# Layer 1 of a two-layer decoder trunk: output projection by token group with Strassen operands made beside it, and the layer-0 handover's operand made in two parts

## The chip, the cores and the metric

The kernel is one program on one core of a Trainium2 chip. The metric is the device time of one execution in microseconds, given as the median of several runs. The engines are TensorE (PE; its weight loads are PEld), VectorE (DVE), ScalarE (ACT), GpSimd (POOL) and SyncE (SP), which issues the DMA transfers.

## The reference

One inference step of a two-layer decoder over 1024 prompt tokens and 64 sample tokens, 1088 in all, width 1024, in float32. What matters here:

```
# layer 0: mixer (causal convolution, stick-breaking attention), FFN
# layer 1: mixer (short gated convolution, causal pooling), FFN
hn  = rms_norm(h, norm_mix_g[1])
mix = concat([c, d]) @ w_out_odd                  # 1024 x 1024, the output projection
h   = h + mix
g, u = split(rms_norm(h, norm_ffn_g[l]) @ w_ffn_in[l])   # 1024 x 2*2816
h   = h + (silu(g) * u) @ w_ffn_out[l]            # 2816 x 1024
y   = rms_norm(h, norm_final_g)
```

## The kernel before

The residual `hb` lies in SBUF as 8 blocks of 128 channels by 1088 tokens. Tokens form group A (`GA`, 0 to 511, one column block of 512), group B (`GB`, 512 to 1087, two of 288) and, in layer 1's mixer, both together (`GT`, blocks of 364, 364 and 360). A float32 product is three matmuls (`mm3`): weight and operand are each a rounded high part and a low part, and the fourth product is dropped. The parts of a weight tile are made as it comes (`w_split`): ACT copies the high part (L177), POOL subtracts for the low part in two halves (L179). Of an operand, ACT makes the high part and DVE the low part (`split`, `prep`, `mix_operand`).

The order on every engine is the program's own. Weights come in the order of the list `seq` through four staging buffers and three buffers `hl`; `w_next` prepares two entries ahead. PSUM holds three accumulators for a single group and two for `GT`. In an FFN, 22 channel groups f are made in pairs, and after each pair from the second on comes the output product of the pair before (eight blocks of 6 matmuls in A, 12 in B, added to `hb` by DVE, L286). The call `slot()` between matmuls is where other work is put in the queues.

A channel group is made in one of two forms. Plain: two products over 8 channel blocks, 48 matmuls in A and 96 in B, with the norm's factor `rr` multiplied in on evacuation (L282). Strassen (`strassen`): seven half-size products for gate and up together, 84 matmuls of 256 or 288 columns, on operands already normed and added ("forms" b11, b21, b22, t1 to t4), and on sums of weight tiles, made by DVE (L193 to L195, L207) and split by ACT and POOL (L189, L190). Here the first five channel groups (`PLAIN`) of three FFNs, layer 0's B and layer 1's A and B, are plain, and `make_forms` makes the forms beside them: DVE norms `hb` (L1372) and takes differences (L1385 to L1388), ACT and POOL split those (L1390, L1391), and `switch` splits the rest with DVE.

The joints that the change touches: `to_mixer` (the last output blocks of layer 0 in group B, with the operand `x1t` of layer 1's mixer made beside them, L1350 and L1352); `run_out` for `GT` (output projection of layer 1, eight groups of 72 matmuls, the last two as a pair, while `prep` makes group A's operand); `channel1` for A, whose last output blocks make group B's operand (`last_a1`); and `channel1` for B. Before the output projection `mix_operand` splits the mixer's output and DMAs the residual back into `hb` from `park`.

Of the kernel before, what the change touches and what calls it, by code (L numbers as in the profile page):

```python
# [8 lines left out]
F = mybir.dt.float32  # L9
# [24 lines left out]
class Grp:  # L34


    def __init__(self, c0, c1, w):
        self.c0, self.c1, self.n, self.w = c0, c1, c1 - c0, w
        self.blocks = [(a, min(a + w, c1 - c0)) for a in range(0, c1 - c0, w)]
        self.t0, self.t1 = c0 // 128, -(-c1 // 128)  # L40
        self.cs = slice(c0, c1)
# [3 lines left out]
GA = Grp(0, HALF, 512)  # L45
GB = Grp(HALF, T, 288)
GT = Grp(0, T, 364)
# [3 lines left out]
def parts(g, acc, *flat):  # L51
    k = sum(b - a == g.w for a, b in g.blocks)
    yield (acc[:, 0:k, :g.w],) + tuple(f[:, 0:k * g.w].rearrange("p (b n) -> p b n", b=k) for f in flat)
    if k < len(g.blocks):
        yield (acc[:, k, :g.n - k * g.w],) + tuple(f[:, k * g.w:g.n] for f in flat)
# [3 lines left out]
def trunk_kernel(ctx, tc, x_prompt, x_sample, cache_k, cache_v, state_conformer, state_shortconv, state_pool,  # L59
# [12 lines left out]

    gstack = ExitStack()
# [12 lines left out]
    par = consts.tile([128, 200], F, name="par")  # L86
# [30 lines left out]
    def add_ffn(l, plain=NF):  # L117
# [13 lines left out]
    PLAIN = 5  # L131
# [14 lines left out]
    for n in range(8):  # L146
        add_in(w_out_odd[0], n * 128)
    for _ in range(2):
        add_ffn(1, PLAIN)

# [110 lines left out]
    def norm_a(g, ps, count):  # L261
        norm_cols(ps, count, g.t0, g.t1)
        k = g.t1 - g.t0
        dg = tmp()
# [104 lines left out]
    def mix_operand(g, x, ks):  # L369
        for c in ks:  # L370
            split(x[c][:, :, :g.n], hb[:, c, g.cs])
# [42 lines left out]
    def run_ffn(g, accs, ps, hidp, x, last, sig=False, slot=lambda: None, forms=None):  # L414
# [3 lines left out]
        gate = {}  # L418

        def ev_g(a):  # L420
            t = tmp()
            scaled(g, t[:, :n], a)
# [7 lines left out]

        def ev_u(f, a):
            t = tmp()
# [3 lines left out]
        def gated(f, t, u):  # L436
            if f // 2 not in hid:
                hid[f // 2] = hidp.tile([128, 2, 2, n], FR, name="hid")
            dst = hid[f // 2][:, f % 2]
# [56 lines left out]
        for q in range(G + 1):  # L496
            if q < G:
                for f in (2 * q, 2 * q + 1):
                    if forms and f >= PLAIN:
                        if f == PLAIN:  # L500
                            forms["switch"]()
                        strassen(f)
                        continue
                    if f == 0:
# [4 lines left out]
                    one(f, 1)  # L509
            if q == G:  # L510
# [53 lines left out]
    x1stack = ExitStack()  # L564
    x1p = x1stack.enter_context(tc.tile_pool(name="x1b", bufs=1, side="right"))
    x1 = [x1p.tile([128, 2, GB.n], FR, name=f"x1_{c}") for c in range(KC)]
# [763 lines left out]
    def to_mixer(hh):  # L1330
        nonlocal x1
        assert not sq and not jobs
        behind = []
        fstack.close()
        x1stack.close()
        gstack.close()
        tmpbox[:] = [tstack.enter_context(tc.tile_pool(name="tmps", bufs=3, side="right")), 1152]
        r1p = r1stack.enter_context(tc.tile_pool(name="r1", bufs=1, side="right"))
        x1 = [r1p.tile([128, 2, T], FR, name=f"x1t_{c}") for c in range(KC)]
        for o in range(2):  # L1340
            h = w_next()
            for i in range(4):
# [404 lines left out]
```

## Time and profile before

| what | us |
|---|---|
| median of 3 runs | 2648.62 (2648.56 to 2649.83) |
| profiled execution, its own time | 2657.19 |
| its span, first to last instruction | 2655.4 |
| TensorE busy in it | 2544.4 |
| DVE, POOL, ACT busy | 1622.3, 1553.1, 1085.1 |

The mean granted clock of TensorE in the profiled execution is 0.985 of full speed. Busy time is an average over stages; what a stage waits for is read in that stage. A matmul lasts longer than the distance to the next, since they are pipelined, so distances are what counts.

### The profile page before, as it was taken

What the parts mean: (1) busy time and instruction counts of PE and PEld (TensorE: products, weight loads), DVE (VectorE), ACT (ScalarE), POOL (GpSimd) and SP (SyncE); (2) the same over time, 40 slices, a digit from 0 to 9 for tenths busy, and PEclk for the clock granted to TensorE, in tenths of its full rate; (3) what the DMA queues carried; (4) which work ended last, traced back from release to release, by engine and by line L of the source; (5) the groups of instructions that cost most, each with busy time, mean ns of one, the idle gap of its engine ahead of it and who ended that gap; (6) DMA issues with size and microseconds to landing.
All of it is one profiled execution on the core that took longest, in us unless ns stands there. A gap on an engine that the chain in (4) does not pass through costs nothing. (4 is left out here: it accounts for less than half of the span.)

```text
span 2655.4 us, 40689 instructions
## 1 busy us (share of the span) xinstructions
PE 2544.4 (96%) x15627; PEld 2263.9 (85%) x15627; DVE 1622.3 (61%) x2262; ACT 1085.1 (41%) x1806; POOL 1553.1 (58%) x1199
## 2 busy tenths in 40 slices
PE   8989999999999999999999999999999998999998
PEld 6788877887666657999999999998788887999997
DVE  4684777868756543377656643332676667676665
ACT  5436766744333324334333421222333334343333
POOL 6756244443333338578787732234778886677775
PEclk9999999999999999999999999999999999999999
DMA  7332231234445442422333321131233333233232
GB/s 215 116 102 71 62 110 40 72 100 129 143 126 161 115 119 88 138 73 80 96 89 87 115 59 48 43 108 40 72 96 96 96 96 94 59 114 107 84 93 76
DMA packets 346009, 254.07 MB, mean 96 GB/s; under 512 B 22657, under 2 KB 295169, under 8 KB 345800
## 3 DMA queue, kind: packets, MB, share of 16 engines
q1 hardware_dynamic: 345784, 251.46, 32.4%
q8 instruction: 124, 2.03, 0.3%
q14 instruction: 69, 0.57, 0.1%
q10 hardware_dynamic: 32, 0.01, 0.0%
HBM read 233.21 MB, written 18.69 MB: 95 GB/s over the span
## 5 line engine op out<-in xcount | busy, mean ns | idle before, releaser
L179 POOL TENSOR_TENSOR hl<-stage,hl 128x512 fp32r<-128x512 f32 x484 | 656.3, 1379 | 485.7 <-ACT hl L177 334.3
L226 PE MATMUL acc<-x,hl 128*128 128x288 f32 (+1 forms) x3792 | 709.8, 340 | 11.8 <-DVE hb L286 7.9
L226 PEld LDWEIGHTS acc<-x,hl 128*128 128x128 f32 x3792 | 585.0, 190 | 98.1 <-issue 38.4
L226 PE MATMUL acc<-hid,hl 128*128 128x288 f32 (+1 forms) x3072 | 554.1, 337 | 26.3 <-DVE tmp L282 13.8
L226 PEld LDWEIGHTS acc<-hid,hl 128*128 128x128 f32 x3072 | 470.1, 191 | 94.4 <-DVE hb L286 15.9
L286 DVE TENSOR_TENSOR hb<-acc,hb 128x512 f32<-128x512 f32 (+2 forms) x376 | 266.7, 718 | 245.8 <-PE acc L226 244.5
L177 ACT ACTIVATE hl<-stage 128x1024 fp32r<-128x1024 f32 x242 | 253.5, 1053 | 213.5 <-PE acc L226 136.8
L463 PE MATMUL acc<-tt,hl 128*128 128x288 f32 (+1 forms) x2448 | 331.6, 291 | 0.5 <-ACT hl L189 0.5
L463 PEld LDWEIGHTS acc<-tt,hl 128*128 128x128 f32 x2448 | 321.0, 189 | 1.7 <-ACT hl L189 0.7
L226 PE MATMUL acc<-x1t,hl 128*128 128x364 f32 (+1 forms) x1728 | 294.7, 332 | 5.5 <-DVE hb L286 5.0
L226 PEld LDWEIGHTS acc<-x1t,hl 128*128 128x128 f32 x1728 | 290.2, 191 | 7.1 <-ACT x1t L1350 5.2
L190 POOL TENSOR_TENSOR hl<-sum,hl 128x512 fp32r<-128x512 f32 x153 | 199.1, 1328 | 158.6 <-ACT hl L189 158.6
L467 DVE TENSOR_TENSOR tmp<-acc,tmp 128x288 f32<-128x288 f32 (+1 forms) x357 | 148.4, 442 | 199.3 <-ACT tmp L479 127.4
L463 PE MATMUL acc<-x,hl 128*128 128x288 f32 (+1 forms) x1836 | 257.1, 292 | 8.3 <-DVE tmp L467 6.5
L463 PEld LDWEIGHTS acc<-x,hl 128*128 128x128 f32 x1836 | 243.8, 190 | 11.2 <-ACT hl L177 5.7
L190 POOL TENSOR_TENSOR hl<-stage,hl 128x512 fp32r<-128x512 f32 x153 | 227.5, 1509 | 18.8 <-ACT hl L189 18.8
L282 DVE TENSOR_TENSOR tmp<-acc,rr 128x512 f32<-128x512 f32 (+3 forms) x128 | 89.6, 711 | 183.0 <-PE acc L226 173.5
L189 ACT ACTIVATE hl<-sum 128x512 fp32r<-128x512 f32 x153 | 87.6, 624 | 209.3 <-DVE sum L195 190.6
L243 POOL TENSOR_TENSOR ss<-ss,tmp 128x512 f32<-128x512 f32 (+2 forms) x62 | 105.7, 1704 | 88.3 <-ACT tmp L242 84.9
L442 POOL TENSOR_TENSOR tmp<-tmp 128x512 f32<-128x512 f32 (+1 forms) x88 | 130.6, 1484 | 24.8 <-ACT tmp L428 23.8
L232 DVE TENSOR_TENSOR hid<-tmp,hid 128x512 fp32r<-128x512 f32 (+1 forms) x88 | 95.7, 1087 | 56.4 <-ACT hid L231 56.0
L226 PE MATMUL acc<-x1a,hl 128*128 128x512 f32 x480 | 122.1, 408 | 3.0 <-POOL hl L179 1.3
(254 smaller groups left out, 2986.7 us busy)
## 6 DMA issues: line engine op xcount, KB each, us to landing
stage<-in_w_ffn_in_dram SPq DMA_DIRECT2D x176, 512.0 KB
stage<-in_w_ffn_out_dram SPq DMA_DIRECT2D x88, 512.0 KB
stage<-in_w_in_even_dram SPq DMA_DIRECT2D x40, 512.0 KB
kst<-in_cache_k_dram SPq DMA_DIRECT2D x64, 256.0 KB
vst<-in_cache_v_dram SPq DMA_DIRECT2D x64, 256.0 KB
stage<-in_w_out_even_dram SPq DMA_DIRECT2D x16, 512.0 KB
stage<-in_w_in_odd_dram SPq DMA_DIRECT2D x16, 512.0 KB
park<-hb SPq DMA_DIRECT2D x16, 288.0 KB
```

The source lines that it names most:

```text
L177: act.activation(hl[:, 0], st, AF.Copy)
L179: pool.tensor_tensor(hl[:, 1, c], st[:, c], f32(hl[:, 0, c]), op=OP.subtract)
L189: act.activation(hl[:, 0, c], x, AF.Copy)
L190: pool.tensor_tensor(hl[:, 1, c], x, f32(hl[:, 0, c]), op=OP.subtract)
L226: pe.matmul(acc[:, b, :c1 - c0], w, x[:, xi, c0:c1], start=first and s == 0, stop=last and s == 2)
L232: dve.tensor_tensor(dst[:, 1], src, f32(dst[:, 0]), op=OP.subtract)
L243: pool.tensor_tensor(ss[:, g.cs], ss[:, g.cs], t[:, :g.n], op=OP.add)
L282: dve.tensor_tensor(d, a, r, op=OP.mult)
L286: dve.tensor_tensor(d, a, d, op=OP.add)
L442: pool.tensor_tensor(t[:, :n], t[:, :n], u[:, :n], op=OP.mult)
L463: pe.matmul(acc[:, :w2], h[:, wi, i, k], xk[:, xi], start=k == 0 and s == 0, stop=k == 3 and s == 2)
L467: dve.tensor_tensor(out, acc[:, :w2], x, op=OP.add)
```

## The change

`GT` gets column blocks of 512, 288 and 288, and an operand of it may be a pair of tiles, one of group A and one of group B (`mm3`, `mix_operand`). At the end of layer 0, group A's part of the mixer's operand is made one output earlier, in the slots of the last output but one (`early`), in memory that the Strassen forms leave; `to_mixer` makes group B's part alone. The output projection of layer 1 runs for group A and then for group B, so its 8 weight tiles are loaded twice. Beside group B's half, `forms_a` norms group A and makes all its forms. Group A's FFN has no plain channel groups; in its slots `forms_b` norms group B, and in its last two outputs `free_a` and `go_on` split that. Group B's FFN has two plain channel groups on that normed operand, without the factor on evacuation (`done`), and the differences are made beside them (`job`).

```diff
-GA = Grp(0, HALF, 512)
-GB = Grp(HALF, T, 288)
-GT = Grp(0, T, 364)
+GA = Grp(0, HALF, (0, 1, 512, 0))
+GB = Grp(HALF, T, (0, 2, 288, 0))
+GT = Grp(0, T, (0, 1, 512, 0), (1, 2, 288, 512))
...
-    for n in range(8):
-        add_in(w_out_odd[0], n * 128)
     for _ in range(2):
-        add_ffn(1, PLAIN)
+        for n in range(8):
+            add_in(w_out_odd[0], n * 128)
+    for _ in range(2):
+        add_ffn(1, PLAIN1[_])
...
+    PLAIN, PLAIN1 = 5, (0, 2)
...
-                pe.matmul(acc[:, b, :c1 - c0], w, x[:, xi, c0:c1],
+                xs, o = (x, 0) if not isinstance(x, tuple) else (x[0], 0) if c0 < x[2] else (x[1], x[2])
+                pe.matmul(acc[:, b, :c1 - c0], w, xs[:, xi, c0 - o:c1 - o],
...
+        done = forms and "switch" not in forms
 
         def ev_g(a):
             t = tmp()
+            if done:
+                for p, o in parts(g, a, t):
+                    act.activation(o, p, AF.Silu)
+                gate["t"] = t
+                return
...
         def ev_u(f, a):
+            if done:
+                t, dst = gate.pop("t"), to_hid(f)
+                for p, o in parts(g, a, t):
+                    dve.tensor_tensor(o, p, o, op=OP.mult)
+                late.append(lambda: split(dst, t[:, :n]))
+                return
...
-                    if forms and f >= PLAIN:
-                        if f == PLAIN:
-                            forms["switch"]()
+                    if f >= plain:
+                        if f == plain:
+                            forms.get("switch", forms.get("ready"))()
                         strassen(f)
                         continue
-                    if f == 0:
+                    if f == 0 and not done:
...
+            if q == G - 1:
+                free()
...
+        x1 = [(x1[c], r1p.tile([128, 2, GB.n], FR, name=f"x1t_{c}"), HALF) for c in range(KC)]
...
-                gain = pc(MIXG + 8 + n)
-                act.activation(x1[n][:, 0], hb[:, n], AF.Copy, scale=gain)
-                for gr in (GB, GA):
-                    lowq.append(lambda gr=gr, n=n, gain=gain: dve.scalar_tensor_tensor(
-                        x1[n][:, 1, gr.cs], hb[:, n, gr.cs], gain, f32(x1[n][:, 0, gr.cs]), op0=OP.mult,
-                        op1=OP.subtract))
-                if n > 1:
-                    behind.append(lowq.pop())
+                prep(GB, [x[1] for x in x1], n, pc(MIXG + 8 + n))
                 low(1)
         low()
-        for f in behind:
-            f()
...
+        ahead = []
+
+        def early():
+            fstack.close()
+            for n in range(KC):
+                def f(n=n):
+                    o, i, gain = x1[n][:, :, :HALF], hb[:, n, GA.cs], pc(MIXG + 8 + n)
+                    act.activation(o[:, 0], i, AF.Copy, scale=gain)
+                    dve.scalar_tensor_tensor(o[:, 1], i, gain, f32(o[:, 0]), op0=OP.mult, op1=OP.subtract)
+                ahead.append(f)
+
         def slot_f():
+            if ahead:
+                return ahead.pop(0)()
...
-    run_out(GT, accs, x1, FFNG + 8, KS, then=(GA, x2))
...
+    def out_fin(g, n, a):
+        added(g, hb[:, n, g.cs], a)
+        add_squares(g, hb[:, n, g.cs], n == 0)
+
+    def normed(out, c, cs, view=lambda ap: ap):
+        dve.scalar_tensor_tensor(out, view(hb[:, c, cs]), pc(FFNG + 8 + c), view(rr[:, cs]), op0=OP.mult, op1=OP.mult)
+
+    def lows(o, src):
+        dve.tensor_tensor(o[:, 1], src, f32(o[:, 0]), op=OP.subtract)
+
+    def sums_t(b11, b12, b21, b22, t1, t2, t3, t4):
+        for o, p, q in ((t1, b12, b11), (t3, b22, b12), (t2, b22, t1), (t4, b21, t2)):
+            dve.tensor_tensor(o, p, q, op=OP.subtract)
+
+    def forms_a(ep):
+        for _ in range(5):
+            yield 1
+        dg = norm_a(GA, ms, D, ep.tile([128, 1024], F, name="fa"))
+        for _ in range(4):
+            yield 1
+        norm_b(GA, ms, dg)
+        for _ in range(2):
+            yield 1
+        w = HALF // 2
+        for k in range(4):
+            fa, fb = (ep.tile([128, 1024], F, name=n) for n in ("fa", "fb"))
+            normed(fa[:, :HALF], k, GA.cs)
+            normed(fa[:, HALF:], k + 4, GA.cs)
+            dsts = ((b1[k][:, :, :w], fa[:, :w]), (b2[k][:, :, :HALF], fa[:, HALF:]),
+                    (xa[k][:, :, :HALF], fb[:, :HALF]), (xa[4 + k][:, :, :HALF], fb[:, HALF:]))
+            for o, i in dsts[:2]:
+                act.activation(o[:, 0], i, AF.Copy)
+            yield 1
+            b11, b12, b21, b22, t2, t1, t4, t3 = (t[:, i * w:i * w + w] for t in (fa, fb) for i in range(4))
+            sums_t(b11, b12, b21, b22, t1, t2, t3, t4)
+            for o, i in dsts[2:]:
+                act.activation(o[:, 0], i, AF.Copy)
+            yield 1
+            yield 1
+            for o, i in dsts:
+                lows(o, i)
+            yield 1
+
+    a0, a1 = pair(GA, accs, xa, KS, {})
+    out_fin(GA, 0, a0)
+    out_fin(GA, 1, a1)
+    for n in range(2, KC):
+        h = w_next()
+        a = accs()
+        block(GA, a, h, xa, KS)
+        out_fin(GA, n, a)
+    with tc.tile_pool(name="fab", bufs=1) as ep:
+        gen = forms_a(ep)
+        for n in range(KC):
+            h = w_next()
+            a = accs()
+            block(GB, a, h, xb, KS, slot=lambda: next(gen, 0))
+            out_fin(GB, n, a)
+            next(gen, 0)
+        for _ in gen:
+            pass
...
+    def forms_b():
+        yield 1
+        dg = norm_a(GB, ms, D)
+        yield 1
+        norm_b(GB, ms, dg)
+        yield 1
+        for k in range(4):
+            normed(xs[k][:, 0:GB.n], k + 4, GB.cs)
+            yield 1
+            normed(xs[k][:, GB.n:], k, GB.cs)
+            yield 1
+
+    def parts_b(k):
+        return [xs[k][:, i * W2:i * W2 + W2] for i in range(4)]
+
+
+    def free_a():
+        def piece(o, i):
+            act.activation(o[:, 0], i, AF.Copy)
+            lows(o, i)
+
+        for k in range(4):
+            seam.append(lambda k=k: piece(b2[k], xs[k][:, 0:GB.n]))
+            seam.append(lambda k=k: piece(b1[k], parts_b(k)[2]))
+
+
+        def last_part(k):
+            if k == 0:
+                rest_b["t"] = hidp1.tile([128, 2, 2, GB.n], FR, name="hid").rearrange(
+                    "p a s (b n) -> p (a s) b n", b=2)
+            piece(rest_b["t"][:, k], parts_b(k)[3])
+
+        for k in range(4):
+            seam.append(lambda k=k: last_part(k))
+
+        def job(k):
+            b21, b22, b11, b12 = parts_b(k)
+            sums_t(b11, b12, b21, b22, b11, b22, b12, b21)
+            for o, x in ((xa[k], xs[k][:, W2:3 * W2]), (xa[4 + k][:, :, R], b12), (xa[4 + k][:, :, L], b21)):
+                act.activation(o[:, 0], x, AF.Copy)
+                pool.tensor_tensor(o[:, 1], x, f32(o[:, 0]), op=OP.subtract)
+
+        jobs.extend(lambda k=k: job(k) for k in range(4))
+
+    def go_on():
+        if seam:
+            seam.pop(0)()
+
+    def ready():
+        while jobs:
+            jobs.pop(0)()
+
+    def channel1(g, last, side, free, plain, x):
+        side = side()
+        turn[0] = 0
+        j0 = wj[0]
...
             turn[0] += 1
-            if turn[0] % 3 == 0:
-                if jobs:
+            if seam:
+                return go_on()
+            if turn[0] % 3 == 0 or turn[0] < 4 and g is GA:
+                if jobs and g is GB:
                     jobs.pop(0)()
-                elif wj[0] > jstart + 2 * PLAIN:
+                elif g is GA or wj[0] > j0 + 2 * plain + 2:
                     next(side, 0)
...
-                prep(GB, x1, n, pc(FFNG + 8 + n))
-                behind.append(lowq.pop())
-                if n < 2:
-                    behind.pop()()
-        for f in behind:
-            f()
-
-
-    def rows_a(fp):
+                go_on()
+        assert not seam
...
+    channel1(GA, last_a1, forms_b, free_a, PLAIN1[0], None)
```

## Rows read from the trace of the kernel before

**Rows 1.** Stretches (us): length, busy of PE, PEld, DVE, ACT, POOL; clock; DMA.

```profile
1508.00:1536.00 28.00, 21.03 (x125) 20.10 (x124) 21.87 (x25) 16.60 (x20) 17.25 (x12) 0.88 0.49 155
1836.00:1856.00 20.00, 16.24 (x67) 12.61 (x66) 7.43 (x15) 6.11 (x9) 10.89 (x6) 0.91 0.18 53
1856.00:1888.00 32.00, 32.00 (x143) 26.50 (x142) 26.51 (x32) 14.04 (x20) 26.57 (x19) 1.00 0.28 82
1888.00:1936.00 48.00, 39.64 (x192) 33.13 (x191) 27.93 (x39) 16.59 (x28) 32.66 (x25) 0.89 0.26 76
2200.00:2224.00 24.00, 18.57 (x67) 13.95 (x67) 15.31 (x16) 7.99 (x12) 10.04 (x9) 0.86 0.29 84
2236.00:2324.00 88.00, 80.35 (x585) 79.20 (x584) 61.35 (x73) 31.18 (x47) 59.40 (x41) 0.98 0.24 69
```

**Rows 2.** VectorE in order of time, layer 0 to 1: start, us, instruction.

```profile
1497.06 0.76 DVE L286 TENSOR_TENSOR hb<-acc,hb 128x576 f32<-128x576 f32 x1 [1.14 <-PE acc L226]
...
1514.59 0.74 DVE L1352 SCALAR_TENSOR_TENSOR x1t<-hb,par,x1t 128x512 fp32r<-128x512 f32 x1
...
1526.66 1.29 DVE L1352 SCALAR_TENSOR_TENSOR x1t<-hb,par,x1t 128x576 fp32r<-128x576 f32 x1
1527.87 0.74 DVE L286 TENSOR_TENSOR hb<-acc,hb 128x576 f32<-128x576 f32 x1
```

**Rows 3.** VectorE's evacuations in layer 1, in order of time.

```profile
1800.65 1.36 DVE L286 TENSOR_TENSOR hb<-acc,hb 128x728 f32<-128x728 f32 x2 [10.64 <-PE acc L226]
...
1920.10 0.69 DVE L282 TENSOR_TENSOR tmp<-acc,rr 128x512 f32<-128x512 f32 x1 [4.75 <-PE acc L226]
...
2312.72 0.76 DVE L282 TENSOR_TENSOR tmp<-acc,rr 128x576 f32<-128x576 f32 x1 [5.64 <-PE acc L226]
```

**Rows 4.** The chain that ended last: start, us, piece.

```profile
2064.16 11.47 PE acc L226 x48
...
2129.81 11.49 PE acc L226 x48
...
2448.30 22.24 PE acc L463 x168
```

**Rows 5.** VectorE in order of time, group A of layer 1.

```profile
1856.12 1.14 DVE L1372 SCALAR_TENSOR_TENSOR xs<-hb,par,rr 128x512 f32<-128x512 f32 x2
...
1882.82 0.42 DVE L1385 TENSOR_TENSOR tmp<-tmp,xs 128x256 f32<-128x256 f32 x1
...
1938.42 0.68 DVE L232 TENSOR_TENSOR hid<-tmp,hid 128x512 fp32r<-128x512 f32 x1
```

**Rows 6.** VectorE by line, 1855 to 1927: busy us, mean ns of one.

```profile
L232 DVE TENSOR_TENSOR x<-xs,x 128x512 fp32r<-128x512 f32 x4 | 4.7, 1232 | 0.0
L1385 DVE TENSOR_TENSOR tmp<-tmp,xs 128x256 f32<-128x256 f32 x4 | 4.6, 1153 | 0.1
...
L1372 DVE SCALAR_TENSOR_TENSOR xs<-hb,par,rr 128x512 f32<-128x512 f32 x4 | 3.4, 848 | 0.0
L1388 DVE TENSOR_TENSOR tmp<-xs,tmp 128x256 f32<-128x256 f32 x4 | 2.7, 671 | 0.1
```

**Rows 7.** GpSimd in order of time, end of group A.

```profile
2193.18 7.55 POOL L179 TENSOR_TENSOR hl<-stage,hl 128x512 fp32r<-128x512 f32 x6
```

**Rows 8.** TensorE in order of time, group A of layer 1.

```profile
1944.76 4.47 PE L463 MATMUL acc<-tt,hl 128*128 128x256 f32 x36
...
1965.12 5.22 PE L226 MATMUL acc<-hid,hl 128*128 128x512 f32 x21
```

**Rows 9.** VectorE in order of time, end of group A.

```profile
2198.31 6.66 DVE L232 TENSOR_TENSOR hid<-tmp,hid 128x512 fp32r<-128x512 f32 x1
```

**Rows 10.** GpSimd by line, 2249 to 2290, start of group B.

```profile
L1391 POOL TENSOR_TENSOR tt<-tmp,tt 128x576 fp32r<-128x576 f32 x8 | 12.3, 1557 | 6.7 <-ACT tt L1390 6.7
```

**Rows 11.** A stretch at the start of the output projection.

```profile
1745.00:1750.00 5.00, 5.00 (x32) 5.00 (x31) 5.00 (x3) 0.00 (x0) 4.41 (x2) 1.00 0.93 326
```

**Rows 12.** VectorE by line, 1935 to 2194, group A's FFN.

```profile
L193 DVE TENSOR_TENSOR sum<-stage 128x512 f32<-128x512 f32 x16 | 32.5, 2031 | 0.0
```

More of the change, by code (lines that the diff above doesn't have):

```diff
@@ L34, with __init__ @@
 class Grp:
-    def __init__(self, c0, c1, w):
-        self.c0, self.c1, self.n, self.w = c0, c1, c1 - c0, w
-        self.blocks = [(a, min(a + w, c1 - c0)) for a in range(0, c1 - c0, w)]
+    def __init__(self, c0, c1, *runs):
+        self.c0, self.c1, self.n, self.runs = c0, c1, c1 - c0, runs
+        self.blocks = [(a + i * w, a + i * w + w) for _, k, w, a in runs for i in range(k)]
         self.t0, self.t1 = c0 // 128, -(-c1 // 128)
@@ L44 @@
 HALF = 512
-GA = Grp(0, HALF, 512)
-GB = Grp(HALF, T, 288)
-GT = Grp(0, T, 364)
+GA = Grp(0, HALF, (0, 1, 512, 0))
+GB = Grp(HALF, T, (0, 2, 288, 0))
+GT = Grp(0, T, (0, 1, 512, 0), (1, 2, 288, 512))
 def parts(g, acc, *flat):
[L52 to L55, printed above, removed]
+    for b, k, w, c in g.runs:
+        yield (acc[:, b:b + k, :w],) + tuple(f[:, c:c + k * w].rearrange("p (b n) -> p b n", b=k) for f in flat)
 @with_exitstack
@@ L70, in trunk_kernel @@
     ctx.enter_context(tc.manual_schedule())
+    x1stack = ExitStack()
+    x1p = x1stack.enter_context(tc.tile_pool(name="x1b", bufs=1, side="right"))
+    x1 = [x1p.tile([128, 2, GB.n], FR, name=f"x1_{c}") for c in range(KC)]
     gstack = ExitStack()
@@ L410, in out_block, with run_ffn @@
             mm3(g, a, h[:, 0, k, i * 128:i * 128 + 128], h[:, 1, k, i * 128:i * 128 + 128], hh[:, k], k == 0, k == 1)
-    def run_ffn(g, accs, ps, hidp, x, last, sig=False, slot=lambda: None, forms=None):
+    def run_ffn(g, accs, ps, hidp, x, last, sig=False, slot=lambda: None, forms=None, plain=NF,
+                free=lambda: None, hw=None):
         G = NF // 2
@@ L436, in gated @@
         def gated(f, t, u):
[L437 to L439 removed]
+            dst = to_hid(f)
             def fin():
@@ L1331, in to_mixer @@
         nonlocal x1
[L1332 to L1335, printed above, removed]
+        assert not sq and not jobs and not ahead
         gstack.close()
+        r1p = r1stack.enter_context(tc.tile_pool(name="r1", bufs=1, side="right"))
+        x1 = [(x1[c], r1p.tile([128, 2, GB.n], FR, name=f"x1t_{c}"), HALF) for c in range(KC)]
         tmpbox[:] = [tstack.enter_context(tc.tile_pool(name="tmps", bufs=3, side="right")), 1152]
-        r1p = r1stack.enter_context(tc.tile_pool(name="r1", bufs=1, side="right"))
-        x1 = [r1p.tile([128, 2, T], FR, name=f"x1t_{c}") for c in range(KC)]
         for o in range(2):
@@ L1424, in trunk_kernel @@
         jstart = wj[0] + 3
-        run_ffn(GB, accs, ms, hidp, x1, to_mixer, slot=slot_f, forms=forms)
+        run_ffn(GB, accs, ms, hidp, x1, to_mixer, slot=slot_f, forms=forms, plain=PLAIN, free=early)
     acc_pool(GT, 2)
@@ L1563, in trunk_kernel @@
+    ystack0 = ExitStack()
+    tstack.close()
     r1stack.close()
[L1564 removed]
+    fp = fstack.enter_context(tc.tile_pool(name="forms1", bufs=1))
     tmpbox[:] = [ystack0.enter_context(tc.tile_pool(name="tmph", bufs=4, side="right")), 640]
[L1566 to L1575 removed]
+    hidp1 = ystack0.enter_context(tc.tile_pool(name="hid1", bufs=2, side="right"))
@@ new lines, in trunk_kernel @@
+    xs = [fp.tile([128, 2 * GB.n], F, name=f"xs{k}") for k in range(4)]
+    L, R = slice(0, W2), slice(W2, GB.n)
+    seam, jobs, rest_b = [], [], {}
+    def forms_b():
[11 more added lines that the diff above has]
+        return [xs[k][:, i * W2:i * W2 + W2] for i in range(4)]
@@ L1589, in end @@
                 pass
-            fstack.close()
+            if g is GB:
+                fstack.close()
             last(hh)
-        run_ffn(g, accs, ms, hidp, x1, end, slot=slot, forms=forms)
-        hstack.close()
+        run_ffn(g, accs, ms, hidp1, x, end, slot=slot, forms=dict(form_views(g.n // 2), ready=ready), plain=plain,
+                free=free, hw=GB.n)
     def last_a1(hh):
-        behind = []
         for o in range(2):
@@ L1706, in to_y @@
         finish(1)
-    channel1(GB, to_y, rows_a)
+    channel1(GB, to_y, rows_a, lambda: None, PLAIN1[1],
+             [(b1[k], rest_b["t"][:, k], W2) for k in range(4)] + b2)
     ystack.close()
```

56 lines of the change are left out of this document (29 added, 27 removed).

## Prediction, made before the changed kernel was run

> **What bounds the kernel now.** I first read busy time and granted clock by stretch. Between the joints TensorE has no idle time: 32.00 of 32.00 us at clock 1.00 in 1856 to 1888 [rows 1]. So the change can win in two ways: fewer or cheaper matmuls, and shorter joints. What a joint loses is its length less busy time times clock: 28 - 21.03 x 0.88 = 9.5 us where layer 0 hands over to layer 1; 20 - 16.24 x 0.91 = 5.2 and 48 - 39.64 x 0.89 = 12.7, together 17.9, where layer 1's FFN starts on group A; 24 - 18.57 x 0.86 = 8.0 at its end; 88 - 80.35 x 0.98 = 9.3 where group B starts [rows 1]. Together 44.7 us. Part of it is clock: at the first joint the idle time is 28 - 21.03 = 7.0, and the other 2.5 us go at the lower of the two levels, 1.2 instead of 2.4 GHz, after the idle time. I then read the engines' instructions in order of time for the price of a column block and for what VectorE (DVE) does at the joints.
>
> **The change part by part**, gains positive.
>
> *A, layer 0 to 1.* Before, ACT makes both groups' operand in the last eight output blocks and DVE its low parts; TensorE's next matmuls need the PSUM tiles that the last add frees. The adds run from 1497.06 to 1527.87 + 0.74 = 1528.6 [rows 2]. After, group A's eight low parts come eight blocks earlier. DVE then has in the first eight blocks 8 adds x 0.68 + 8 low parts x 1.0 (an estimate between 0.74 and 1.29 [rows 2]) + two hidden splits of some 0.75 = 14.9 us, in the last eight, up to the last add, 8 x 0.68 + 6 x 1.1 = 12.0: the last add ends near 1497.1 + 26.9 = 1524.0, 4.6 us earlier, while TensorE's 16 blocks of 12 matmuls need 16 x 6.40/4 = 25.6 [rows 3]. I take 5, with a little of the clock; ends 0 (all low parts at 1.29 push the last add back to 1528) and 9.5 (the whole loss).
>
> *B, column blocks.* 1088 columns become 512 + 288 + 288 for 364 + 364 + 360; the count of matmuls stays. 72 matmuls of the old form took 10.64 + 1.36 = 12.00 us (DVE's idle time until their block ends, and the evacuation, so the time from one to the next), so three take 0.500; 24 of 512 took 4.75 + 0.69 = 5.44, so 0.2267 each; 48 of 288 took 5.64 + 0.76 = 6.40, so 0.1333 each [rows 3]. 0.2267 + 0.2667 = 0.4934, and 576 triples x 0.0066 = 3.8. Ends 0 and, with 22.24/168 = 0.1324 for 288 [rows 4], 4.9.
>
> *C, the start of group A's FFN.* Gone are the pair at the end of the output projection with its operand, the norm that waits for the squares, and the forms made beside five plain channel groups: the 17.9 us. In their place forms_a runs inside group B's half of the projection, 8 x 6.40 = 51.2 us, and the first Strassen product needs all of it. By its yields the first piece stands behind the third add, at 3 x 6.40 + 0.75 = 19.9 us; behind it come 4 x 10 DVE instructions with two SBUF inputs, 3 for the first weight sums, and 5 more adds (3.8): 23.7 us beside the 43. Undisturbed, one k costs 1.14 (two of 512) + 4 x 0.42 + 3 x 0.68 + 0.42 = 5.3 [rows 5]; with POOL 83% busy (26.57 of 32) [rows 1] the same kinds took 2 x 0.848 + 4 x 0.91 (mean of the first and last difference) + 3 x 1.232 + 0.42 = 9.5 [rows 6]. In group B's half POOL has two weight halves and one square, 3 x 1.45 = 4.35 of 6.40 us, 68%, so I interpolate to 8.7 for a k and 1.13 for a weight sum: 34.8 + 3.4 + 23.7 = 61.9, that is 10.7 us after TensorE is done. With 2.5 for the clock, as at the first joint, 17.9 - 13.2 = 4.7 is won. Ends: undisturbed, 21.1 + 2.0 + 23.7 = 46.9 fits and all 17.9 is won; at the full contended price 65.2, 14.0 late, 1.4 won. Queued behind the late forms: on DVE the adds that free PSUM (three buffers, so two blocks or 12.8 us of slack), on ACT the copies that wait for them and behind these the weight copies of two blocks later, on POOL the halves that wait for those.
> Six POOL halves in a row took 7.55 us, 1.26 each [rows 7]. The Trainium skill, SBUF — State Buffer, section "SBUF: two separate sides", says that DVE (with two SBUF inputs) and GpSimd take a shared port pair as an exclusive lock for a whole instruction. By it the times would simply add: 23.1 of DVE + 15 x 1.26 of POOL + 23.7 = 65.7, 14.5 late, and 3.8 less is won than by the rows; the stretch of [rows 6] does not decide it, so it is a rival.
>
> *D, group A's five plain channel groups.* A plain one is 2 x 5.44 = 10.88 [rows 3], two by Strassen in a row took 1965.12 - 1944.76 = 20.36, so 10.18 each [rows 8]: 5 x 0.70 = 3.5. But a round of two Strassen groups and one output takes (2129.81 - 2064.16)/2 = 32.8 [rows 4] against 20.36 + 10.88 = 31.2: 1.6 lost at each output, where weight sums hold DVE. Two outputs more of that kind, less some slack: I take 1; ends -1.3 and 3.5.
>
> *E, the end of group A.* Twelve small copies and subtractions stand in the last two outputs instead of eight wide ones in and behind the last. A two-input split of 0.68 took 6.66 us here [rows 9], against the train of [rows 7], which stays: the same two output and two input weights are prefetched. I leave most of the 8.0 standing and take 2; ends -4 (the twelve at the contended price) and 6.
>
> *F, the start of group B.* Norm and normed operand are already made in group A's time; two plain groups (25.6 us) remain, with four jobs beside them, the last issued some 19 us in. Each has four differences and on POOL three low parts; the 576-wide kind took 1.557 [rows 10], the three about 3.2. With the weights POOL has about 4 x 3.2 + 12 x 1.4 = 29.6 us for 25.6. The forms may be late by 0 to 4; I take 3 of the 9.3 as staying: 6; ends 0 and 9.3.
>
> *G, group B's three plain ones.* 2 x 6.40 = 12.8 against 22.24/2 = 11.12 [rows 3, 4]: 3 x 1.68 = 5.0.
>
> *H, at nothing or nearly.* Eight more weight loads: one ACT copy and two POOL halves (2.5) for 5.44 us of TensorE, covered; without cover 2.5 each. The restored residual is needed sooner: the DMA engines are 93% busy there [rows 11], the first add comes 10.9 us after the first matmul, and three PSUM buffers give 10.9 more; a late one costs its lateness. The operand is split beside a pair that now takes a k in 1.36 us, while its two low parts take 0.68 and some 0.74 and more with POOL at 4.41 of 5 [rows 5, 11]: -1; ends 0 and -4.
>
> Sum: 5 + 3.8 + 4.7 + 1 + 2 + 6 + 5 - 1 = 26.5 us. The profiled execution took 2657.19 us (span 2655.4), so 2630.7; it stands 8.6 above the median of the runs, 2648.62, from which I get **2622**.
>
> **Rivals.** *The forms are hidden (0.19).* Places where POOL is idle between weights are long enough, and DVE catches up: the 10.7 and the clock fall away, 13.2 more, 2609. For it: 46.9 is under 51.2. Against: POOL's share there is 68%.
> *The lock adds up (0.12)*: 3.8 less, 2626, by the rule named under C.
> *The joints refill (0.11).* A, E and F give nothing since the same low parts stand in the same DVE queue, only earlier: 13 less, 2635. For it: DVE was busy 21.87 of 28 and 61.35 of 88 us there [rows 1].
> *Slower (0.12).* One mechanism: DVE starves in group B's half of the projection, so that the first Strassen product waits. The sum of two weight tiles took 2.03 us on average in group A's FFN [rows 12], three times the 0.68. It decides at the point where forms are 31.8 us later than forecast (26.5 and the 5.3 that a measurement can tell): ready at 93.7, so (93.7 - 23.7)/43 = 1.63 us for each of the 43. At 2.03 they are ready at 111, 59.8 late, and the time is 2671. Against it: such a price needs a POOL instruction beside every DVE one, and POOL has 15 for 43.
> *No change to be told (0.06)*: refilled joints and forms some 20 late together.
>
> **How the numbers follow.** The forecast has 0.40, with 2614 to 2631 of its own. The cases on the faster side sum to 0.82, same 0.06, slower 0.12; same means within 0.2% (5.3 us), about what a measurement of this kernel can tell from no change. The best ends together give 56, the worst about -1; the range takes in hidden forms and refilled joints, with their bounds, and stops where no change begins: 2604 to 2643.
>
> **What would show it.** Right: TensorE's granted clock stays 1.00 at the first joint, and its idle time there is under 4 us; the 1088 columns take 0.493 a triple; one gap of about 10 us before the first Strassen product of group A, ended by a DVE low part; no gap over 2 us in the first output of group B. Wrong: the gap before group A's Strassen is nil (then faster than forecast) or over 30; TensorE waits for weight halves in the first four Strassen groups in a row, which POOL must feed without an output between; or the wait at the residual's DMA.

## The result, and the profile after

The changed kernel took 2657.00 us (median of 10 runs), the kernel before 2650.82 beside it: ratio 1.0025, 95% interval 1.0014 to 1.0036. In a second measurement (e13 below) it took 2656.19 against 2655.99: 1.0003, 0.9992 to 1.0015. So it is no faster, and at most 0.4% slower by the outer end of the intervals; 2622 us were forecast.

The profiled execution took 2656.81 us (span 2655.0) against 2657.19 (2655.4) before, the latter 6.4 above the median of its runs, so the pair of traces shows about 6 us less loss than the medians. The table gives the time from the start of one phase on TensorE to the start of the next in both traces, in us, and sets it against the prediction's steps:

| stretch (steps) | before | after | gain | forecast |
|---|---|---|---|---|
| second last output of layer 0 to the mixer's first matmul (A) | 33.49 | 34.57 | -1.08 | +5 |
| mixer to the start of group A's FFN (B, H) | 309.71 | 312.51 | -2.80 | +2.8 |
| from there to group A's tenth output (C, D) | 356.10 | 359.82 | -3.72 | +5.7 |
| group A's last two outputs (E) | 31.06 | 34.80 | -3.74 | +2 |
| group B's FFN up to its last output (F, G) | 398.28 | 386.43 | +11.85 | +11 |

The parts ahead of and behind these come to 0.11 worse, which makes the 0.4 us between the spans. One row held; four came out lower by 27 us in all.

Stretches of the changed kernel, in the columns of [rows 1]:

```profile
1508.00:1536.00 28.00, 21.96 (x133) 20.91 (x132) 20.50 (x23) 12.90 (x19) 18.33 (x12) 0.88 0.47 153
1842.00:1874.00 32.00, 23.03 (x133) 20.59 (x132) 22.91 (x30) 13.71 (x24) 23.85 (x18) 0.76 0.23 66
2202.00:2237.00 35.00, 25.87 (x100) 19.14 (x99) 26.70 (x30) 14.84 (x26) 19.21 (x15) 0.90 0.27 77
2237.00:2324.00 87.00, 83.29 (x628) 82.61 (x628) 63.98 (x81) 37.09 (x63) 75.64 (x57) 1.00 0.32 94
```

Group B's start is all but full: 3.7 us idle in 87 at clock 1.00, where 7.7 in 88 were idle. Group A's start is the worst: busy 23.03 of 32 at 0.76. TensorE in order of time shows what ended each wait (in brackets: idle us, releaser). First the waits of the kernel before at the same places, then those of the changed kernel:

```profile
1528.76 17.98 PE L226 MATMUL acc<-x1t,hl 128*128 128x364 f32 x90 [5.03 <-DVE hb L286]
1838.47 7.09 PE L226 MATMUL acc<-x,hl 128*128 128x512 f32 x30 [1.60 <-ACT hl L177]
2205.63 7.70 PE L226 MATMUL acc<-hid,hl 128*128 128x512 f32 x22 [3.76 <-DVE hb L286]
```

```profile
1513.95 13.51 PE L232 MATMUL acc<-hid,hl 128*128 128x288 f32 x88 [3.82 <-DVE hid L238]
1529.68 0.47 PE L232 MATMUL acc<-x,hl 128*128 128x512 f32 x1 [2.22 <-DVE hb L292]
1740.80 4.91 PE L232 MATMUL acc<-x,hl 128*128 128x512 f32 x19 [1.54 <-DVE tmp L288]
1746.28 1.67 PE L232 MATMUL acc<-x,hl 128*128 128x512 f32 x6 [0.56 <-DVE x L238]
1748.64 11.75 PE L232 MATMUL acc<-x,hl 128*128 128x512 f32 x49 [0.69 <-DVE x L238]
1761.49 4.72 PE L232 MATMUL acc<-x,hl 128*128 128x512 f32 x19 [1.11 <-POOL hl L183]
1842.19 0.39 PE L488 MATMUL acc<-x,hl 128*128 128x256 f32 x2
1844.77 1.82 PE L488 MATMUL acc<-x,hl 128*128 128x256 f32 x8 [2.19 <-POOL hl L194]
1847.34 3.78 PE L488 MATMUL acc<-x,hl 128*128 128x256 f32 x16 [0.75 <-DVE x L1602]
1852.38 2.50 PE L488 MATMUL acc<-x,hl 128*128 128x256 f32 x10 [1.27 <-POOL hl L194]
1870.10 2.40 PE L280 MATMUL m<-tmp,ones 128*128 128x512 f32 x4 [4.41 <-DVE tmp L271]
2213.23 8.56 PE L232 MATMUL acc<-hid,hl 128*128 128x512 f32 x28 [5.30 <-DVE hb L292]
2232.23 1.67 PE L232 MATMUL acc<-hid,hl 128*128 128x512 f32 x6 [1.39 <-DVE hb L292]
```

None of these is the one gap of 10 us that was forecast. Most are ended by something that stands in an in-order queue behind other work. At 1513.95 it is the split of the last hidden tile into its high and low part, whose ScalarE half was done at 1505.9; on VectorE it stands behind the eight early low parts (first and last shown), and the last add ends at 1529.5, not at 1524.0:

```profile
1498.08 1.28 DVE L1437 SCALAR_TENSOR_TENSOR x<-hb,par,x 128x512 fp32r<-128x512 f32 x1 [0.43 <-ACT x L1436]
...
1511.07 1.09 DVE L1437 SCALAR_TENSOR_TENSOR x<-hb,par,x 128x512 fp32r<-128x512 f32 x1
1512.09 1.81 DVE L238 TENSOR_TENSOR hid<-tmp,hid 128x576 fp32r<-128x576 f32 x1
...
1528.80 0.74 DVE L292 TENSOR_TENSOR hb<-acc,hb 128x576 f32<-128x576 f32 x1
```

At group A's start ScalarE idles 4.39 us for an add (L292) that VectorE does behind the forms, and the next weight copy (L193) stands behind that square:

```profile
1843.63 0.63 ACT L1636 ACTIVATE x<-fb 128x512 fp32r<-128x512 f32 x1 [0.83 <-DVE fb L1606]
1848.65 0.68 ACT L248 ACTIVATE tmp<-hb 128x576 f32<-128x576 f32 x1 [4.39 <-DVE hb L292]
1849.24 0.62 ACT L193 ACTIVATE hl<-sum 128x512 fp32r<-128x512 f32 x1
```

The 4.41 at 1870.10 is the norm of group B, which the change moved into group A's time: TensorE reaches the matmuls that spread it while VectorE's short chain is still under way.

### The profile page after: what moved, and what is told of

The parts are those of the page before. It is cut to its first block, busy times and chain, and to the rows that moved or that the text cites. A ratio compares the mean times of both kernels' runs of the same rounds, so it can differ in the third digit from the quotient of the medians.

```text
span 2655.0 us, 41261 instructions
## 1 busy us (share of the span) xinstructions
PE 2538.9 (96%) x15771; PEld 2239.7 (84%) x15771; DVE 1656.6 (62%) x2328; ACT 1107.9 (42%) x1878; POOL 1601.4 (60%) x1240
## 3 DMA queue, kind: packets, MB, share of 16 engines
q1 hardware_dynamic: 354104, 255.66, 32.8%
## 5 line engine op out<-in xcount | busy, mean ns | idle before, releaser
L232 PE MATMUL acc<-x,hl 128*128 128x512 f32 (+1 forms) x3648 | 791.9, 353 | 16.4 <-DVE hb L292 10.1
L232 PEld LDWEIGHTS acc<-x,hl 128*128 128x128 f32 x3648 | 587.7, 191 | 102.9 <-issue 37.9
L292 DVE TENSOR_TENSOR hb<-acc,hb 128x512 f32<-128x512 f32 (+1 forms) x376 | 267.9, 718 | 209.4 <-PE acc L232 205.3
L488 PE MATMUL acc<-x,hl 128*128 128x288 f32 (+1 forms) x2628 | 360.8, 292 | 8.7 <-POOL hl L194 5.6
L488 PEld LDWEIGHTS acc<-x,hl 128*128 128x128 f32 x2628 | 346.5, 190 | 11.8 <-POOL hl L194 7.0
L488 PE MATMUL acc<-b,hl 128*128 128x256 f32 (+1 forms) x1512 | 209.1, 290 | 10.3 <-DVE tmp L492 9.4
L232 PE MATMUL acc<-x1t,hl 128*128 128x288 f32 x1152 | 217.0, 296 | 0.0
L232 PEld LDWEIGHTS acc<-x1t,hl 128*128 128x128 f32 x1152 | 197.0, 189 | 17.9 <-issue 0.5
L488 PEld LDWEIGHTS acc<-b,hl 128*128 128x128 f32 x1512 | 196.8, 189 | 14.4 <-ACT hl L193 10.6
L193 ACT ACTIVATE hl<-sum 128x512 fp32r<-128x512 f32 x177 | 101.4, 623 | 229.9 <-DVE sum L199 207.2
L249 POOL TENSOR_TENSOR ss<-ss,tmp 128x512 f32<-128x512 f32 (+1 forms) x69 | 111.8, 1620 | 86.6 <-ACT tmp L248 83.3
L193 ACT ACTIVATE hl<-stage 128x512 fp32r<-128x512 f32 x177 | 103.7, 618 | 70.7 <-PE acc L232 64.7
```

The source lines that it names most:

```text
L193: act.activation(hl[:, 0, c], x, AF.Copy)
L232: pe.matmul(acc[:, b, :c1 - c0], w, xs[:, xi, c0 - o:c1 - o], start=first and s == 0, stop=last and s == 2)
L249: pool.tensor_tensor(ss[:, g.cs], ss[:, g.cs], t[:, :g.n], op=OP.add)
L292: dve.tensor_tensor(d, a, d, op=OP.add)
L488: pe.matmul(acc[:, :w2], h[:, wi, i, k], xk[:, xi], start=k == 0 and s == 0, stop=k == 3 and s == 2)
```

## The experiments

Theory 1: each lost stretch is a wait made by a place in a queue, and goes when that place is changed with the work left as it is. Theory 2, the prediction's "joints refill": VectorE and GpSimd are over-booked there, and what is taken away comes back. Lengths are differences of starts on TensorE; where the code of a stretch was not touched they varied by execution: the handover (first row of the table) 34.3 to 35.6, start of A (first matmul to first output) 61.4 to 62.8, end of A (its last two outputs) 32.1 to 34.8. Ratios are against the kernel before, with 95% intervals.

**e1: the norm of group B one step later** (`yield 1` added between `norm_a` and `norm_b` in `forms_b`; the scale kept in `xs[3]`).

> The changed kernel, with one step of group B's second norm moved: the spread of its scale over the partitions (two matmuls that wait for VectorE's short chain) is issued at the end of the third Strassen group of group A's feed-forward part instead of at the second slot of the second one. Theory 1 (the lost time is single waits made by places in in-order queues): TensorE's wait of 4.41 us at 1870.10 goes, with the granted clock of 0.50 and 0.77 behind it, so group A's stretch up to its first output falls from 61.9 to 56 +- 1 us and the ratio to the kernel before from 1.0025 to 1.000. Theory 2 (VectorE and GpSimd are over-booked where the stages meet, so a wait that is removed comes back behind the next operation): the wait moves, the stretch stays at 61.9 +- 1.5 and the ratio at 1.0025.

Start of A 58.41, 3.5 less; the wait at the spread is gone, one of 3.17 for Strassen's adds stands at 1870.51. Ratio 1.0011 (0.9996 to 1.0025). Theory 1 gave the gap and the clock behind it some 6 us; 3.5 were won, so the outcome lies between the theories.

**e2: the split of the last hidden tile (the hidden split) after four of the eight early pieces.**

```
-  if o == 0 and i == 1:
+  if o == 0 and (i == 1 or i == 3 and q == G - 1 and g is GB and not done):
       flush()
```

> The changed kernel, with the split of the last hidden tile of layer 0's second feed-forward part issued after four of the eight early operand pieces instead of after all eight. Theory 1: the tile is split by 1509, TensorE's wait of 3.82 us at 1513.95 goes, and the handover from the second last output to the mixer's first matmul falls from 34.57 to 30 to 31 us; ratio 1.0010. Theory 2: the same low parts stand in the same queue, the last add ends at 1529 +- 1 all the same, and the handover stays between 33.5 and 34.6; ratio 1.0025.

Handover 32.34. The 3.82 is gone, and a wait of 2.00 for an add behind the early pieces has come in its place:

```profile
1507.98 15.87 PE L232 MATMUL acc<-hid,hl 128*128 128x288 f32 x108 [2.00 <-DVE hb L292]
1526.29 0.47 PE L232 MATMUL acc<-x,hl 128*128 128x512 f32 x1 [2.43 <-DVE hb L292]
```

Ratio 1.0022 (1.0007 to 1.0037). The length lies between the two forecasts: both theories have a part here.

**e3: squares and norm behind the weight copies.** In group B's half only blocks 0 to 4 call `add_squares` at once; `forms_b` does the last three at its first step and begins the norm two steps later than it did.

> The changed kernel, with the squares of the last three blocks of group B (ScalarE, and their sums on GpSimd) issued after the weight copies of the first Strassen groups, and group B's norm moved behind them (its two steps at the end of the third and in the fifth group). Theory 1: of the stretch from group A's first feed-forward matmul to its first output, 61.9 us, the norm's wait (4.41) and the waits for weights at 1844 to 1852 (2.19, .75, 1.27) shrink, 53 to 55 us are left; ratio 0.9985 to 0.9995. Theory 2: VectorE's forms bound the start, the waits come back behind the forms and the stretch stays at 59 or more; ratio 1.0015 to 1.0025. A third theory, that GpSimd cannot split the weights of four Strassen groups in a row: the waits move to the second and third group, in sum as long as now.

Start of A 54.92; what is left is mainly the forms, with the lower clock behind them (the stretch 1844 to 1852 at 0.57). Ratio 0.9988 (0.9975 to 1.0001).

```profile
1840.80 1.21 PE L488 MATMUL acc<-x,hl 128*128 128x256 f32 x8 [0.64 <-POOL hl L194]
1845.86 5.83 PE L488 MATMUL acc<-x,hl 128*128 128x256 f32 x26 [3.85 <-DVE x L1602]
```

**e4: the twelve operand pieces at the end of group A (`seam`) later, each low part one piece behind its copy.**

```
+  seam.extend([lambda: None] * 4)
   def piece(o, i):
       act.activation(o[:, 0], i, AF.Copy)
-      lows(o, i)
+      low(0)
+      lowq.append(lambda: lows(o, i))
...
+  low(0)
```

> The changed kernel, with the twelve operand pieces at the end of group A's feed-forward part begun four slots later, after GpSimd's run of weight halves, and each low part issued one piece behind its copy, so that no add on VectorE stands behind a low part that waits for ScalarE. Theory 1: no low part is held for 7.62 us, TensorE's wait of 5.30 us at 2213.23 and those of .81, 1.39 and 1.40 go, the end of group A falls from 34.94 to 29 to 31 us; ratio 1.0005. Theory 2: twelve low parts in the last half of the stretch hold the adds instead, or group B's first matmuls wait for them; end of group A and start of group B together lose as much as now; ratio 1.0025.

End of A 26.90, below what either theory gave; one wait of 2.46 for the hidden split remains. Group B's start took 1.4 more and the rest of it 0.5. Ratio 1.0010 (0.9998 to 1.0023).

**e5: e2, and the last eight adds before group B's low parts 2 to 7** (the `behind` list of the kernel before, put back).

> The changed kernel with the earlier split of the last hidden tile (as in the run e2_hid_first, where the handover was 32.34 us) and, as in the kernel before, the low parts of group B's operand chunks 2 to 7 issued on VectorE behind all eight last adds instead of one after each add. Theory 1 (places in queues): the eight adds are no longer spaced by low parts of 1.1 to 1.35 us, the accumulators come free at TensorE's pace, and the handover falls to 28 to 29.5 us. Theory 2 (VectorE over-booked): the mixer's first matmuls then wait for the low parts, and handover and wait together stay at 32 to 33.

Handover 31.13, between the theories: the wait ahead of the mixer fell from 2.43 to 0.94, that of 2.00 stayed. In e8, with the same code, it was 29.64; there the joint was granted clock 1.00, here 0.94. Ratio 0.9995 (0.9982 to 1.0008).

**e6: the low parts in another form** (`scalar_tensor_tensor(out, src, 1.0, high, mult, subtract)` in `lows`).

> The changed kernel, with the low parts of the layer 1 operands (28 in group A's forms, 12 at the seam) issued as scalar-tensor-tensor operations (source times 1.0 minus high part) instead of tensor-tensor subtractions; values, sizes and order are the same. If VectorE is held by GpSimd whatever the form of the two-input operation, nothing changes: 7.62 us for the first seam low part, 34.8 us for the end of group A, 61.9 from its start to its first output. If the hold belongs to the tensor-tensor form, as the rows of layer 0's early pieces hint (1.09 to 1.28 us for 512 columns beside GpSimd in scalar-tensor-tensor form, 1.58 to 1.78 in tensor-tensor form), the first seam low part takes 1.0 to 1.5 us, the end of group A falls to 29 to 31, and the start by 1 to 3; ratio 0.9995 to 1.0005.

The first seam low part took 1.46 us, but it did so in tensor-tensor form as well, in e1 and five more of the runs: my hint does not hold (one of layer 0's early pieces, at 1501.06, took 1.92 us too). The forms cost the same (1501 against 1499 ns for 512 columns, 1232 against 1228 for 256). Start of A 61.58; ratio 1.0023 (1.0007 to 1.0038).

**e7: the projection's operand splits by group**, all of A's before all of B's in `mix_operand`, the residual loaded by halves.

> The changed kernel, with the operand splits of layer 1's output projection ordered by group: all of group A's before group B's, each followed by the load of that half of the residual, instead of group A and group B in turn for each chunk. Theory 1: TensorE's waits of .56 and .69 us for the splits, VectorE's of 1.05 and 1.31 for the residual and TensorE's of 1.11 for weights whose copy stands behind the squares of those adds go; group A's half of the projection falls from 48.4 to 46 +- .5, ratio 1.0015. Theory 2: the splits of group B then stand in front of the first adds and hold as much: 48 or more.

Group A's half of the projection 46.67 for 48.44, close to theory 1; the waits of .56, .69 and 1.11 became one of 1.14. Ratio 1.0011 (0.9997 to 1.0025).

**e8: e3, e4 and e5 together.**

> The changed kernel with four re-orderings together: squares behind the weight copies and the later norm (as in e3_weights_first), the seam pieces later and their low parts one piece behind (e4_seam_later), the hidden split earlier and the last adds before the low parts (e5_adds_first). Theory 1: the stretches are apart in time, so what each gave alone adds up: start of group A 55 us, its end 27, handover 28 to 30, in all 17 to 20 us below the changed kernel, ratio 0.995 to 0.996. Theory 2: what one order gives back is taken up again at the next stage; ratio 0.998 or more.

2641.88 us, ratio 0.9959 (0.9943 to 0.9974): start of A 55.77, end 26.92, handover 29.64. Stretch by stretch they add up.

**e9: the forms begun one block earlier** (in `forms_a` 3 steps, norm, 3 steps, spread, 1 step for 5, 4 and 2).

> The changed kernel, with group A's norm and the making of its forms begun four slots, one block of the output projection (6.6 us), earlier; nothing else is moved. If the forms' end on VectorE sets the start of group A's feed-forward part, as the prediction had it (10.7 us late), the stretch up to the first output falls from 61.9 to 53 to 56 us. If the places in the queues set it (weight copies behind squares, the norm's spread), the forms are ready in time and the stretch stays at 59.5 or more, because the waits of 2.19, 1.25 and 4.41 us stay: about 1 us is gained from the wait of .75 to 1.37 us for a form; ratio 1.002.

Start of A 57.57, between the two ranges, but group B's half of the projection rose from 52.95 to 54.96: 2.4 won in all. The norm's wait stood as it was (4.42) and weights held the first products. Ratio 1.0001 (0.9993 to 1.0010).

**e10: e8, e9, e7 and the early hidden split in all four feed-forward parts** (the condition on group and form dropped).

> The four re-orderings of e8_all_order, with the forms begun one block earlier (as in e9_forms_sooner), the projection's operand splits ordered by group (e7_halves_apart), and the earlier hidden split at the end of layer 1's group A too. In e8_all_order the start of group A still waited 3.85 us for a form, with the granted clock at 0.57 behind it. If what is left there is the forms' lateness, the start falls from 55.8 to 48 to 51, and with 1.5 to 2 from the projection the ratio is 0.992 to 0.993. If VectorE is over-booked there, the forms that start earlier hold the adds of the projection and the start stays at 54 or more; ratio 0.995 or above.

2637.17 us against 2654.31, ratio 0.9938 (0.9924 to 0.9951), below both kernels by more than the intervals, though not the 0.992 to 0.993 expected. The end of A fell to 23.18, its start only to 52.63, where weights now hold:

```profile
1855.95 0.47 PE L490 MATMUL acc<-b,hl 128*128 128x256 f32 x2 [1.38 <-ACT hl L193]
1859.13 2.50 PE L490 MATMUL acc<-b,hl 128*128 128x256 f32 x10 [2.70 <-POOL hl L194]
```

**e11: e10 with all low parts in e6's form.**

> The kernel of e10_all_sooner, with all low parts of operands and hidden tiles that were tensor-tensor subtractions issued in scalar-tensor-tensor form. In e6_one_form the first seam low part took 1.46 us instead of 7.62, and GpSimd's six weight halves beside it 8.53 instead of 7.55. If the hold of VectorE still costs something after the re-ordering, 1 to 4 us are gained against e10_all_sooner; if GpSimd's halves, which then take longer, hold the weights instead, nothing or 1 to 2 us are lost.

2640.25 us, ratio 0.9949 (0.9936 to 0.9962): not to be told from e10.

**e12: the column blocks alone, in the kernel before** (only `Grp`, the three groups and `parts` taken over).

> The kernel before, with only the column blocks of the whole token range changed (512, 288, 288 instead of 364, 364, 360): part B of the prediction alone. By its price, .0066 us on each of 576 triples, the mixer's input phase (384 triples) falls by 2.5 and the output projection (192) by 1.3, in all 3.8 us; ratio 0.9986. If the unequal blocks cost as much at the evictions as they save in the matmuls, the ratio is 0.9995 to 1.0005.

Ratio 0.9999 (0.9987 to 1.0011); from the mixer's first matmul to group A's first 309.76 us for 309.71. The 3.8 us are not there. A mixer period, four output blocks or 96 triples, can be read between two transposes, first in the kernel before, then here:

```profile
1655.87 0.27 PE L1506 MATMUL m<-ident,st 120*128 120x120 f32 x1
...
1669.38 0.77 PE L1544 MATMUL m<-pp,pwp 128*128 128x360 f32 x3 [0.17 <-ACT hb L1546]
...
1706.66 0.27 PE L1506 MATMUL m<-ident,st 120*128 120x120 f32 x1
```

```profile
1654.20 0.27 PE L1505 MATMUL m<-ident,st 120*128 120x120 f32 x1
...
1668.01 0.66 PE L1543 MATMUL m<-pp,pwp 128*128 128x288 f32 x3 [0.38 <-ACT hb L1545]
...
1705.10 0.27 PE L1505 MATMUL m<-ident,st 120*128 120x120 f32 x1
```

50.79 and 50.90 us, in the changed kernel 50.77 (1655.42 to 1706.19), where 96 x 0.0066 = 0.6 less was forecast; the wait at the pooled product grew from 0.17 to 0.38. What a triple itself costs shows where two output blocks follow each other without other work of TensorE: the distance of their evacuations is 24 triples, 12.00 us before and 11.96 here (11.92 in the changed kernel, 1637.74 to 1649.66), where 0.16 less was forecast:

```profile
1638.07 1.36 DVE L282 TENSOR_TENSOR tmp<-acc,rr 128x728 f32<-128x728 f32 x2 [1.50 <-PE acc L226]
1650.07 1.36 DVE L282 TENSOR_TENSOR tmp<-acc,rr 128x728 f32<-128x728 f32 x2 [8.32 <-PE acc L226]
```

```profile
1636.46 1.35 DVE L281 TENSOR_TENSOR tmp<-acc,rr 128x512 f32<-128x512 f32 x2 [1.49 <-PE acc L225]
1648.42 1.35 DVE L281 TENSOR_TENSOR tmp<-acc,rr 128x512 f32<-128x512 f32 x2 [8.29 <-PE acc L225]
```

**e13 and e14: the changed kernel again, and both edits at group A's start (e3 and e9) alone.**

> The changed kernel unaltered, beside e14_start_only. If ratios of different calls can be set side by side it comes out at 1.0025 within its interval (1.0014 to 1.0036) again, and the start of group A at 61.4 to 62.8 us. If the ratio depends on the call by more than the interval, it comes out at 1.0010 or below, and gains under 4 us in the other runs are then to be read from their traces alone.

> The changed kernel with both edits at the start of group A's feed-forward part and nothing else: squares and norm behind the weight copies (e3_weights_first, 7.0 us less from group B's half of the projection to the first output) and forms begun one block earlier (e9_forms_sooner, 2.4 less). If the two causes are independent the two stretches together fall from 114.9 to 105.5 +- 1. If GpSimd's weight halves for four Strassen groups in a row are the next bound, what the earlier forms free is taken up by waits for weights: 107 to 108.5, as in e10_all_sooner (107.4).

The control gave 1.0003 (0.9992 to 1.0015), the start of A 61.69. Its interval meets the first one only at its edge, so from one measurement to the next the ratio moves by about 0.2%, and the small gains above rest on the traces. e14 took 2647.76 us, ratio 0.9969 (0.9958 to 0.9979). The two stretches fell from 114.9 to 106.6 (54.74 + 51.84): 8.3 of 9.4, just outside the range for independent causes, and the waits for weights that e10 had, 1.39 and 2.71, are here too. The two causes mostly add; the weights are next.

## Why the prediction was wrong

*A failed.* It summed VectorE's work in the last sixteen output blocks and put the end of the sum at 1524. For the first eight it had 14.9 us where the trace has 17.0, so the sum wasn't far off, but the hidden split that TensorE needs for the last output was counted at some 0.75 without its place, behind all eight early pieces. Moved up (e2) and with the adds ahead of the low parts (e5, e8), 2.4 to 3.9 us are won against before: most of the 5 was there, but not with this order.

*B failed as a term.* Its 0.2267 for 512 columns is one distance in a feed-forward product [rows 3] and does not hold elsewhere. In the changed kernel's projection 512-wide matmuls run alone, at granted clock 1.00, and from one block of 24 to the next it is 5.62 us, 0.234 each:

```profile
1772.58 0.69 DVE L292 TENSOR_TENSOR hb<-acc,hb 128x512 f32<-128x512 f32 x1 [4.94 <-PE acc L232]
1778.20 0.69 DVE L292 TENSOR_TENSOR hb<-acc,hb 128x512 f32<-128x512 f32 x1 [4.93 <-PE acc L232]
```

With 2 x 0.1333 that is 0.501 a triple, no gain on the projection's 192. In the mixer a triple took 0.500 us before, 0.498 in e12 and 0.497 in the changed kernel, so at best half of the 0.0066; in e12 the longer wait at the pooled product takes that back. Why the same width costs 0.227 in one place and 0.234 in another stays open.

*C was mis-sized, the largest miss.* Its work was priced a little high: from the start of group B's half (1789.24) to the end of the last low part (1847.9) it took 58.7 us for 61.9, about 5.7 late for 10.7. The Trainium skill, SBUF — State Buffer, "SBUF: two separate sides", by which whichever side starts first has the shared ports for its whole instruction, had led to an estimate of 65.7; this trace is below both, and that rival's sum has fallen. But the step ends at the forms. It names the weight copies queued behind them and gives that no price, though waits for weight halves in the first four Strassen groups stand among its own signs of being wrong, and it doesn't see that group B's norm, which F counts as saved, is now waited for here. The waits for weights and norm (2.19, 1.27, 4.41) and the clock at 0.76 make the start lose 21 us (61.9 against 4 x 10.18) for the 13.2 forecast. Re-ordering gave back 7.0 (e3), earlier forms 2.4 (e9), both 8.3 (e14).

*D was lost in part.* The later rounds of two Strassen groups and one output took 32.5 us for 32.8 [rows 4], but the first two behind the start took 35.0 and 34.5 (1904.12 to 1939.16 to 1973.67). In them VectorE does seven of the eight operations by which `forms_b` norms group B, and TensorE waits for Strassen's adds:

```profile
1908.25 1.84 DVE L1599 SCALAR_TENSOR_TENSOR xs<-hb,par,rr 128x576 f32<-128x576 f32 x1
1926.90 1.67 PE L488 MATMUL acc<-b,hl 128*128 128x256 f32 x12 [1.35 <-DVE tmp L492]
```

That is 4.5 us, and no order gave it back: e8 and e10, which begin the norm later, have 33.7, 35.0 and 33.7 or 33.8 before 32.5 again. No run takes the norm out of these rounds, so this cause is read from the traces only.

*E failed:* -3.7 for +2, and -1.0 to -2.0 in most other traces of this code (last section). The low parts stood in front of the adds. With the pieces later and behind (e4), 26.9, 4 better than before, of which group B gave 1.9 back: about the 2 that I took were to be had.

*F and G held:* 11.9 for 11, with no gap over 1.4 us in group B's first Strassen groups and 3.7 us idle at its start.

*H came near its size.* With B at nothing, -2.8 for -1 in the pair of traces; 1.5 of that is the clock at the mixer's start (last section), and in the control the same stretch takes 311.10, which is -1.4. The waits of 1.54 (the switch of PSUM tiles), .56, .69 and 1.11 make 3.9; group by group splits (e7) take 1.8 off that.

In the number, nearest was the case given 0.06, no change to be told. It has refilled joints and forms some 20 us late together: the start of group A did lose 21, but with forms only 5.7 late. Of the joints of the rival "they refill" (2635), A and E came out below nothing and F held. That rival is right on A and E and mostly wrong on why: most of the work fits. e8 and e10 leave all of it in, and by their ratios, set against the changed kernel's two, they are 12 to 17 and 17 to 23 us faster. Only 2.00 us at the first joint, the weight halves at group A's start and the 4.5 under D came back as theory 2 has it. The mechanism of "slower" did not come: in group B's half the weight sums took 0.68 us each, not 2.03. And the worst ends as listed add to -2.9 us, not to about -1, which changes nothing here.

Open are the two prices of 512 columns under B, and the 6 us between the pair of profiled executions and the medians. e12's trace, a kernel within 0.1% of before, is 2.3 us shorter than that of before in group A's FFN (384.86 for 387.16) and 1.7 ahead of the handover; the rest is not placed.

## What to carry to other kernels

When work is moved next to a stage's end, summing busy time per engine isn't enough: for each thing that TensorE waits for, write down what is issued ahead of it on its engine, and on the engine that feeds that one. A step that is moved takes its waits along, so the place it goes to needs a price too. And a distance between matmuls that is read in one place need not hold in another, not even for the same width: one small run of the stream that is meant is worth more than a sum of such readings.

## What was not expected of the hardware

A VectorE low part beside six GpSimd weight halves takes very different times, with the code around it the same. In the changed kernel's first trace it took 7.62 us and the six ran at 1.26 each; in e1 1.45, with the six at 1.42 each (and so in the control, e2, e3, e5 and e7). e9 had 7.62 again, and e14 lay between, with 2.69 and 1.35:

```profile
2204.86 7.62 DVE L1602 TENSOR_TENSOR b<-xs,b 128x576 fp32r<-128x576 f32 x1 [0.40 <-ACT b L1692]
```

```profile
2200.64 7.55 POOL L183 TENSOR_TENSOR hl<-stage,hl 128x512 fp32r<-128x512 f32 x6
```

```profile
2196.54 1.45 DVE L1602 TENSOR_TENSOR b<-xs,b 128x576 fp32r<-128x576 f32 x1 [0.40 <-ACT b L1693]
```

```profile
2192.31 8.54 POOL L183 TENSOR_TENSOR hl<-stage,hl 128x512 fp32r<-128x512 f32 x6
```

The price at the joint is only about 2 us (end of A 34.8 and 34.5 with 7.62, 33.6 in e14, 32.1 to 33.0 else), since with 1.45 TensorE waits 3.48 us for the hidden split a little later.

The clock, too, differs with the code unchanged. After the same waits of 3.82 and 2.22 us the changed kernel's next stretch was granted 0.73, that of e3 1.00; from the mixer's first matmul to the output projection's first it took 211.1 us in the one and 209.6 in the other. Of the traces with the code unchanged up to there, e4, e9 and e14 also have 211.1, and e1, e6, e7 and the control 209.5 to 209.6:

```profile
1529.68:1532.68 3.00, 3.00 (x13) 2.73 (x14) 2.18 (x2) 1.36 (x2) 2.84 (x3) 0.73 0.61 196
```

```profile
1528.98:1531.98 3.00, 3.00 (x18) 2.73 (x19) 2.18 (x2) 1.35 (x2) 2.84 (x3) 1.00 0.62 192
```
